# Two-part tokens evicted straight from PSUM: one change to a two-layer transformer kernel

## The chip, the cores and the metric

The kernel runs on one core of a Trainium2 chip. The metric is device time in microseconds (us) of one execution, as the median of several. TensorE (PE) multiplies and transposes and writes PSUM; ScalarE (ACT) and VectorE (DVE) read PSUM and SBUF; GpSimd (POOL) works on SBUF alone; SyncE (SP) issues most transfers.

## The reference

256 tokens of 1024 values pass through two layers, all in float32. The part that the change touches lies between the mixers and the experts. Each layer has a mixer (a block attention in the first layer, a compressed, selected and windowed attention, `nsa`, in the second), a feed-forward layer, a gated embedding term, and then a hybrid attention and a mixture of experts. Each of these begins with a norm:

```python
def _rms(x, g):
    xf = x.astype(F32)
    y = xf * lax.rsqrt(jnp.mean(xf * xf, axis=-1, keepdims=True) + RMS_EPS)
    return (y * g.astype(F32)).astype(x.dtype)
```

The feed-forward layer is down(silu(gate(y)) * up(y)) with 2816 hidden values. The embedding term adds sigmoid(y @ w_gate) * (p @ w_proj), where p holds 256 values per token.

## The kernel before, in words

The tokens are two tiles of 128 rows in `h` (tile t, 1024 columns). Products need the tokens the other way round, so each norm ends in a turn: `Norm.norm` writes the normed rows `xn`, and `Norm.turn(t)` lets TensorE transpose the eight 128-column chunks into two PSUM banks of four chunks each and evicts them with the gain.

A float32 product is made of three products of a shorter type: every operand is held in two parts, a high part and a low part (value minus high part). `mm3` (lines 329 to 331) multiplies high by high, high by low and low by high. For tokens these are the tiles XH and XL, written by `turn`. For weights, `Split` makes the parts: ScalarE casts a piece of 1024 columns into `whi` (line 193), and `Split.lows` subtracts it on an engine `second` into `wlo` (line 201). `Split.get(job)` hands out a piece; with `ahead` it first casts as many further pieces as there are free places (`pump`), and then it issues every low part that is pending. `second` is VectorE, but GpSimd within `ple` and for four pieces in layer 1's hybrid attention.

In `turn` before, ScalarE evicts bank 0 and VectorE bank 1, each in four instructions with the gain, back into `xn` as float32 (lines 378 and 382). ScalarE then casts chunks 0 and 1, 2 and 3, and 4 to 7 into XH (line 373), and VectorE subtracts the same three pieces into XL (line 386). Eight norms run through it, two tiles each, sixteen turns in all; the norms of the expert layers have no low part and keep their form.

The order of work is the order in which the program issues it: nothing reorders instructions of an engine, and each engine works through its own in order. The places of the sixteen turns:

- the start of the kernel (the first mixer's input, not normed: `raw`);
- `last_steps` of each mixer: the rest of the output product, then `ple_product` twice (the embedding's projection, twelve matmuls each, copied to `pv` by ScalarE at line 868), then both turns, and then the feed-forward layer with ten weight pieces cast and subtracted ahead;
- the end of `ffn` (tile 0) and the start of `ple` (tile 1);
- the end of `ple` (tile 0) and the start of what follows it (tile 1): the second mixer, or layer 0's hybrid attention;
- layer 1's hybrid attention (both).

`ple` is the gate block: for each tile eight pieces of product, at two of them a sigmoid on ScalarE (line 943), a multiplication with `pv` and an addition to `h` on VectorE (lines 946 and 390), the sums of squares on ScalarE (line 342) and at the end the norm.

In the second mixer's attention, `proj_steps` works a projection in four steps between units of attention; three of them fetch with `ahead`. In the hybrid attention, `halves` squares each half of the output on ScalarE and adds the second square to the first on GpSimd (line 1350).

Of the kernel before, what the change touches and what calls it, by code (L numbers as in the profile page):

```python
# [10 lines left out]
F32 = mybir.dt.float32  # L11
# [3 lines left out]
AF = mybir.ActivationFunctionType  # L15
ALU = mybir.AluOpType
# [3 lines left out]
D = 1024  # L20
# [133 lines left out]
class Split:  # L154


    def __init__(self, nc, ring, size):
        self.nc, self.ring, self.size = nc, ring, size
        self.jobs, self.at, self.made, self.free, self.low, self.pools = [], {}, {}, [], [], []
        self.second = nc.vector  # L160
        self.spare = 1

    def add(self, job, key, view, last):

# [8 lines left out]
    def make(self, spare=0):  # L173

        n = len(self.made)
        name, key, view, last = self.jobs[n]
        for pool, bufs, until, live in self.pools:
            while live and self.free[live[0]]:
                live.pop(0)
            if len(live) < bufs - spare and (until is None or n < self.at[until]):  # L180
                break
        else:
            return False
        live.append(n)
        src = view(self.ring.get(key))
        hi = pool.tile([128, self.size], F32R, name="whi", tag="whi", bufs=bufs)
        lo = pool.tile([128, self.size], F32R, name="wlo", tag="wlo", bufs=bufs)
        shape = [int(v) for v in src.shape[1:]]
        vh, vl = hi[:, :int(np.prod(shape))], lo[:, :int(np.prod(shape))]
        if len(shape) == 2:  # L190
            vh = vh.rearrange("p (a b) -> p a b", a=shape[0])
            vl = vl.rearrange("p (a b) -> p a b", a=shape[0])
        self.nc.scalar.copy(vh, src)  # L193
        self.made[name] = (vh, vl)
        self.low.append((self.second, vl, src, vh, key if last else None))
        return True

    def lows(self):

        for eng, vl, src, vh, key in self.low:  # L200
            eng.tensor_sub(vl, src, vh)  # L201
            if key:
                self.ring.done(key)
        self.low = []

    def pump(self, most=99):

# [3 lines left out]
    def get(self, job, ahead=True):  # L211
        while job not in self.made:
            assert self.make(), job
        if ahead:
            self.pump()
        self.lows()
        return self.made[job]

    def done(self, job):
# [41 lines left out]
def tile_kernel(ctx: ExitStack, tc: tile.TileContext, x, out, cat, sat, stop=None):  # L261
    nc = tc.nc
# [70 lines left out]
    class Norm:  # L333
# [26 lines left out]

        def turn(self, t, raw=False):
            src = h[:, t] if raw else self.xn[t]
            xn = tmp.tile([128, D], F32, name="xn", tag="xn") if raw else self.xn[t]
            pts = [wps(), wps()]
            for k in range(8):
                nc.tensor.transpose(pts[k // 4][:, 128 * (k % 4):128 * (k % 4) + 128], src[:, 128 * k:128 * k + 128], ident)

            to = [self.to[:, t, k] if self.low is None else xn[:, 128 * k:128 * k + 128] for k in range(8)]
            f_ = [slice(128 * c, 128 * c + 128) for c in range(4)]

            def parts(a, b):
                v = xn[:, 128 * a:128 * b].rearrange("p (c n) -> p c n", n=128)
                nc.scalar.copy(self.to[:, t, a:b], v)  # L373
                return self.low[:, t, a:b], v, self.to[:, t, a:b]

            lows = []
            for c in range(4):
                nc.scalar.activation(to[c], pts[0][:, f_[c]], AF.Copy, scale=self.gain[:, c:c + 1])
                if c % 2 and self.low is not None:
                    lows.append(parts(c - 1, c + 1))  # L380
            for c in range(4):
                nc.vector.tensor_scalar(to[4 + c], pts[1][:, f_[c]], self.gain[:, 4 + c:5 + c], None, ALU.mult)
            if self.low is not None:
                lows.append(parts(4, 8))
            for o, v, hi in lows:
                nc.vector.tensor_sub(o, v, hi)  # L386

    def add_half(t, b, v, nxt):
        hs = h[:, t, 512 * b:512 * b + 512]
# [93 lines left out]
    with ExitStack() as c1:  # L483
# [80 lines left out]
            plan_moe(l)  # L564


        def proj(name, b, nq, pair=None, skew=None, mid=None, bank=acc, ahead=True):


            o = [bank(), bank()]  # L570
            xh, xl = pair or (XH, XL)

            def piece(q, t):
                vh, vl = split.get((name, b, q), ahead)
                for c in range(2):
                    k = 2 * q + c
                    mm3(o[t], xh[:, t, k], xl[:, t, k], vh[:, c, :], vl[:, c, :], k == 0, k == 2 * nq - 1)

            if skew:
                for t in range(2):  # L580
                    for q in range(nq):
                        if q == nq - 1 and t == 0:
                            skew()
                        piece(q, t)
                        if q == nq - 1 and t and mid:
                            mid()
                        if t:
                            split.done((name, b, q))
                        if q % 2:
                            side.tick()  # L590
                    yield t, o[t]
                return
            for q in range(nq):
                for t in range(2):
                    piece(q, t)
                split.done((name, b, q))
                side.tick()
            yield 0, o[0]
            yield 1, o[1]

        def proj_steps(key, end):
# [259 lines left out]
                nc.vector.tensor_sub(pp[1][:, t], v, pp[0][:, t])  # L861
                yield 0

        def ple_product(i, b, pp, pv):

            for t, o in proj(f"pp{i}", b, 1, pp, bank=wps, ahead=False):
                pv[b, t] = keep.tile([128, 512], F32, name="pv", tag="pv", bufs=4)
                nc.scalar.copy(pv[b, t], o)

        def last_steps(i, outp, nxt, pp, pv):  # L870
            fns = [lambda: outp.finish(nxt, T1[10 + 6 * i]), lambda: ple_product(i, 0, pp, pv), lambda: ple_product(i, 1, pp, pv),
                   lambda: nxt.turn(0), lambda: nxt.turn(1)]
            for k in sorted(range(len(fns)), key=lambda k: T1[11 + 6 * i + k]):
                fns[k]()

        def ffn(i, nm, nxt):
            down = [[acc(), acc()] for _ in range(2)]
# [43 lines left out]
        def ple(i, nm, pv, nxt):  # L921

            seq = [(b, q) for b in range(2) for q in range(4)]
            split.second = nc.gpsimd
            for t in range(2):
                for n, (b, q) in enumerate(seq):
                    if t == 0 and n == T1[0]:
                        nm.turn(1)
                    if t and n == T1[1]:
                        nxt.turn(0)  # L930
                    if q == 0:
                        o = acc()
                    vh, vl = split.get((f"pg{i}", b, q), t == 0 or n < 6)
                    if n == T1[2]:
                        nxt.half(t, 0)
                    for c in range(2):
                        k = 2 * q + c
                        mm3(o, XH[:, t, k], XL[:, t, k], vh[:, c, :], vl[:, c, :], k == 0, k == 7)
                    if t:
                        split.done((f"pg{i}", b, q))  # L940
                    if q == 3:
                        sg = ptile([128, 512], F32, "sgp")
                        nc.scalar.activation(sg, o, AF.Sigmoid)
                        if b:
                            nc.scalar.preload_act_table_set(EXP)
                        nc.vector.tensor_mul(sg, sg, pv[b, t])
                        add_half(t, b, sg, b and nxt)
                nxt.norm(t)
            split.second = nc.vector

        rows_d = dram.tile([24, 383], F32, name="rows_d")
        cbias = keep.tile([128, 2, 16, 16], F32, name="cbias")
# [146 lines left out]
        def nsa(nm, nxt):  # L1099
# [140 lines left out]
            fill = proj_steps(("nsa", 1), lambda o: side.later(T1[6], lambda: side.spawn(second(o))))  # L1240
            side.later(T1[7], lambda: side.spawn(blocks(0)))
            att.hold()
            next(fill)
            for _ in att.start():
                next(fill)
                side.tick()
            att.run(AT1)
            side.drain()
            outp.chunk(6, (1,))
            last_steps(1, outp, nxt, pp, pv)  # L1250
# [18 lines left out]
    with ExitStack() as c2:  # L1269
# [41 lines left out]
        def mixer(l, qkv, sq, yh, yl):  # L1311
# [31 lines left out]
            def halves(br, c, y, gain, n):  # L1343

                if c == 0:
                    nc.scalar.activation(sq[:, br], y, AF.Square)
                else:
                    s_ = ptile([128, S], F32, "sqc", bufs=1)
                    nc.scalar.activation(s_, y, AF.Square)
                    nc.gpsimd.tensor_add(sq[:, br], sq[:, br], s_)  # L1350
                g = gain[:, c:c + 1]
                nc.scalar.activation(yh[:, br, c], y, AF.Copy, scale=g)
                yield n
                nc.vector.scalar_tensor_tensor(yl[:, br, c], y, g, yh[:, br, c], ALU.mult, ALU.subtract)
# [602 lines left out]
```

## Time and profile before

| | |
|---|---|
| median of 3 runs | 1916.67 us (1911.02 to 1917.64) |
| profiled execution | 1910.32 us, of it span 1908.5 us |
| mean granted TensorE clock | 0.974 of full speed |
| busy share of the span: PE, DVE, ACT, POOL | 93%, 42%, 35%, 4% |
| experts of the two layers | about 860 to 1315 and 1400 to 1908 us of the span |

In a row of a timeline stand the start and the duration in us, engine, line, operation, the tiles out<-in, their shape (partitions by elements) and the number of instructions joined in the row; in brackets is the idle time of the engine before it and what ended that. A row that joins several instructions gives the time from the first one's start to the last one's end. A row of a group gives the number of instructions, their busy time in us, the mean of one in ns, and the idle time ahead of them. A row of windows gives the stretch and its length, then for each engine (PE, its weight loads, DVE, ACT, POOL) busy us and instructions, then the granted clock, the busy share of the DMA queues and GB/s.

### The profile page before, as it was taken

How to read it: one execution, taken by the hardware profiler on the slowest of the kernel's cores; microseconds unless marked ns; L12 is line 12 of the kernel's file. 1: busy time of each engine (PE TensorE's matmuls, PEld its weight loads, DVE VectorE, ACT ScalarE, POOL GpSimd, SP SyncE). 2: the span in 40 equal slices, each digit the busy share in tenths (PEclk: the TensorE clock that was granted, in tenths of full speed). 3: DMA queues.
4: the chain of work that ended last, by engine and by line, in shares of the span. 5: the costliest groups of instructions: out<-in, count | busy, mean ns of one | idle time of the engine just before them, and what ended most of it. 6: DMA issues, size and time to landing. Idle time of an engine off the chain costs nothing. (4 is left out here: it accounts for less than half of the span.)

```text
span 1908.5 us, 25241 instructions
## 1 busy us (share of the span) xinstructions
PE 1777.5 (93%) x9983; PEld 1169.5 (61%) x9983; DVE 811.0 (42%) x1772; ACT 674.4 (35%) x1371; POOL 69.1 (4%) x92
## 2 busy tenths in 40 slices
PE   8998999898999999999999978997999999978996
PEld 6778999786689997874444443443874444433442
DVE  6667455767775556872111111113773111111112
ACT  6656445646574446651111110113552111110111
POOL 0000000300000003000000000001010000000000
PEclk9999999999999999999999989998998999998998
DMA  8437555442255554749999999999649999999996
GB/s 299 154 125 244 203 188 193 131 160 66 95 177 199 199 191 134 267 164 396 421 421 421 420 421 378 422 420 385 223 155 374 420 421 421 420 420 377 421 421 279
DMA packets 152908, 555.76 MB, mean 291 GB/s; under 512 B 9872, under 2 KB 69712, under 8 KB 103632
## 3 DMA queue, kind: packets, MB, share of 16 engines
q1 hardware_dynamic: 150672, 546.45, 73.9%
q0 software_dynamic: 2112, 7.63, 1.2%
q8 instruction: 81, 1.33, 0.3%
q14 instruction: 43, 0.35, 0.1%
HBM read 552.96 MB, written 1.09 MB: 290 GB/s over the span
## 5 line engine op out<-in xcount | busy, mean ns | idle before, releaser
L1745 PE MATMUL wps<-wring,h 128*64 128x512 f32 x1936 | 454.0, 596 | 10.6 <-DMA wring<-in_w_expert_up_dram 7.9
L1745 PEld LDWEIGHTS wps<-wring,h 128*64 128x64 f32 x1936 | 150.0, 138 | 287.3 <-issue 258.6
L201 DVE TENSOR_TENSOR wlo<-wring,whi 128x1024 fp32r<-128x1024 f32 (+1 forms) x273 | 288.3, 1094 | 73.6 <-ACT whi L193 73.3
L193 ACT CAST whi<-wring 128x1024 fp32r<-128x1024 f32 (+1 forms) x283 | 254.8, 945 | 23.0 <-PE acc L331 12.0
L329 PE MATMUL wps<-xh,whi 128*128 128x256 f32 x832 | 236.5, 284 | 4.7 <-ACT xh L373 4.7
L330 PE MATMUL wps<-xl,whi 128*128 128x256 f32 x832 | 234.8, 282 | 1.3 <-DVE xl L386 1.3
L331 PE MATMUL wps<-xh,wlo 128*128 128x256 f32 x832 | 234.5, 282 | 0.0
L1780 PE MATMUL wps<-wring,aT 128*64 128x512 f32 x984 | 227.4, 597 | 0.0
L1758 DVE SCALAR_TENSOR_TENSOR a<-wps,gs,a 128x256 f32<-128x256 f32 x64 | 28.0, 479 | 369.8 <-PE wps L1745 369.8
L329 PEld LDWEIGHTS wps<-xh,whi 128*128 128x128 f32 x832 | 157.5, 189 | 10.5 <-ACT xh L373 5.2
L1789 DVE SCALAR_TENSOR_TENSOR yl<-wps,gs,yh 128x512 fp32r<-128x512 f32 x64 | 47.9, 750 | 267.8 <-ACT yh L1788 263.9
L331 PEld LDWEIGHTS wps<-xh,wlo 128*128 128x128 f32 x832 | 160.3, 193 | 0.0
L330 PEld LDWEIGHTS wps<-xl,whi 128*128 128x128 f32 x832 | 157.5, 189 | 3.2 <-DVE xl L386 1.8
L329 PE MATMUL acc<-whi,xh 128*128 128x512 f32 (+1 forms) x360 | 146.6, 407 | 3.3 <-ACT whi L193 3.3
L1780 PEld LDWEIGHTS wps<-wring,aT 128*64 128x64 f32 x984 | 70.8, 137 | 128.4 <-issue 123.0
L331 PE MATMUL acc<-whi,xl 128*128 128x512 f32 (+1 forms) x360 | 141.3, 392 | 8.5 <-DVE xl L386 8.5
L330 PE MATMUL acc<-wlo,xh 128*128 128x512 f32 (+1 forms) x360 | 141.4, 393 | 2.3 <-DVE wlo L201 2.3
L1788 ACT ACTIVATE yh<-wps,gs 128x512 fp32r<-128x512 f32 x64 | 43.8, 687 | 262.9 <-PE wps L1780 212.2
L1769 ACT COPY aT<-wps 128x256 f32<-128x256 f32 x32 | 11.9, 372 | 239.7 <-PE wps L1768 239.7
L1755 ACT ACTIVATE a<-wps,gs 128x512 f32<-128x512 f32 x32 | 22.0, 688 | 179.9 <-PE wps L1745 179.9
L331 PEld LDWEIGHTS acc<-whi,xl 128*128 128x128 f32 x360 | 69.8, 194 | 24.9 <-DVE xl L386 10.2
L329 PEld LDWEIGHTS acc<-whi,xh 128*128 128x128 f32 x360 | 70.1, 195 | 18.1 <-ACT whi L193 4.6
(374 smaller groups left out, 2424.5 us busy)
## 6 DMA issues: line engine op xcount, KB each, us to landing
wring<-in_w_expert_down_dram SPq DMA_DIRECT2D x123, 1024.0 KB, 19.8
wring<-in_w_expert_up_dram SPq DMA_DIRECT2D x122, 1024.0 KB, 19.8
wring<-in_w_expert_gate_dram SPq DMA_DIRECT2D x120, 1024.0 KB, 19.8
wring<-in_w_ffn_gate_dram SPq DMA_DIRECT2D x22, 1024.0 KB, 9.1
wring<-in_w_ffn_up_dram SPq DMA_DIRECT2D x22, 1024.0 KB, 5.4
wring<-in_w_ffn_down_dram SPq DMA_DIRECT2D x22, 1024.0 KB, 7.4
wring<-in_w_in_dram SPq DMA_DIRECT2D x18, 1024.0 KB, 8.6
wring<-in_w_in_ab_dram SPq DMA_DIRECT2D x10, 1024.0 KB, 8.7
```

The costliest lines, as they stand in the source:

```text
L193: self.nc.scalar.copy(vh, src)
L201: eng.tensor_sub(vl, src, vh)
L329: nc.tensor.matmul(o, lh, rh, start=start, stop=False)
L330: nc.tensor.matmul(o, lh, rl, start=False, stop=False)
L331: nc.tensor.matmul(o, ll, rh, start=False, stop=stop)
L1745: nc.tensor.matmul(o[i][64 * ab:64 * ab + 64, :], xg[:, k, at:at + 64], ws[ab][:, c, :], start=k == 0, stop=k == 7)
L1755: nc.scalar.activation(a, o[0], AF.Silu, scale=r)
L1758: nc.vector.scalar_tensor_tensor(a[:, s_], o[1][:, s_], r, a[:, s_], ALU.mult, ALU.mult)
L1769: (nc.vector.tensor_copy if hf else nc.scalar.copy)(aT[:, 2 * hf:2 * hf + 2], pt[:, 256 * hf:256 * hf + 256].rearrange("p (j n) -> p j n", ...
L1780: nc.tensor.matmul(y[d2][64 * ab:64 * ab + 64, :], aT[:, 2 * hf + j, 64 * ab:64 * ab + 64], ws[ab][:, j, 512 * d2:512 * d2 + 512], start=h ...
L1788: nc.scalar.activation(ys[0][:, s_], y[d2], AF.Copy, scale=g)
L1789: nc.vector.scalar_tensor_tensor(ys[1][:, s_], y[d2], g, ys[0][:, s_], ALU.mult, ALU.subtract)
```

## The change

`turn` no longer goes through `xn`. For every chunk ScalarE evicts bank to XH with the gain, rounded to the high part, and VectorE takes the same chunk of the bank once more, multiplies it by the gain, subtracts the high part and writes XL:

```diff
-            for c in range(4):
-                nc.scalar.activation(to[c], pts[0][:, f_[c]], AF.Copy, scale=self.gain[:, c:c + 1])
-                if c % 2 and self.low is not None:
-                    lows.append(parts(c - 1, c + 1))
...
+            for c in range(8):
+                v = pts[c // 4][:, 128 * (c % 4):128 * (c % 4) + 128]
+                g, to = self.gain[:, c:c + 1], self.to[:, t, c]
+                if self.low is not None:
+                    nc.scalar.activation(to, v, AF.Copy, scale=g)
+                    nc.vector.scalar_tensor_tensor(self.low[:, t, c], v, g, to, ALU.mult, ALU.subtract)
+                elif c < 4:
+                    nc.scalar.activation(to, v, AF.Copy, scale=g)
+                else:
+                    nc.vector.tensor_scalar(to, v, g, None, ALU.mult)
```

In `last_steps` the order of the products stays, and turn 0 is issued between the two tiles' matmuls of the last one (`proj` gets a parameter `between` for that):

```diff
-            fns = [lambda: outp.finish(nxt, T1[10 + 6 * i]), lambda: ple_product(i, 0, pp, pv), lambda: ple_product(i, 1, pp, pv),
-                   lambda: nxt.turn(0), lambda: nxt.turn(1)]
-            for k in sorted(range(len(fns)), key=lambda k: T1[11 + 6 * i + k]):
-                fns[k]()
+            outp.finish(nxt, T1[10 + 6 * i])
+            ple_product(i, 1 - i, pp, pv)
+            ple_product(i, i, pp, pv, lambda: nxt.turn(0))
+            nxt.turn(1)
```

```diff
             for q in range(nq):
                 for t in range(2):
                     piece(q, t)
+                    if between and t == 0:
+                        yield 0, o[0]
+                        between()
```

The low parts of the gate blocks' pieces go to VectorE, and so do the hybrid attention's added squares:

```diff
         def ple(i, nm, pv, nxt):
-            split.second = nc.gpsimd
...
-            split.second = nc.vector
```

```diff
                     nc.scalar.activation(s_, y, AF.Square)
-                    nc.gpsimd.tensor_add(sq[:, br], sq[:, br], s_)
+                    nc.vector.tensor_add(sq[:, br], sq[:, br], s_)
```

In the second mixer's attention `split.late` is set from before the first step of the projection until the attention has run. A fetch with it issues the low parts that were pending before it looked ahead, and leaves those of the pieces that it has just cast to the next fetch. `make` also issues pending low parts first where the piece's weights are not in the ring yet:

```diff
     def get(self, job, ahead=True):
         while job not in self.made:
             assert self.make(), job
+        n = len(self.low) if self.late else None
         if ahead:
             self.pump()
-        self.lows()
+        self.lows(n)
```

## Rows read from the trace of the kernel before

**Rows 1.** Windows of the span: busy us by engine, granted clock, DMA share, GB/s

```profile
525.00:545.00 20.00, 17.11 (x88) 15.03 (x87) 16.32 (x33) 17.16 (x38) 0.38 (x2) 0.83 0.10 30
```

**Rows 2.** Groups by shape over the span: xcount, busy us, mean ns, idle before

```profile
L378 ACT ACTIVATE xn<-wps,sm 128x128 f32<-128x128 f32 x48 | 15.0, 363 | 10.7 <-PE wps L366 10.7
L382 DVE TENSOR_SCALAR xn<-wps,sm 128x128 f32<-128x128 f32 x48 | 13.5, 343 | 11.7 <-PE wps L366 11.5
L1354 DVE SCALAR_TENSOR_TENSOR yl<-wps,sm,yh 128x256 fp32r<-128x256 f32 x8 | 3.8, 478 | 0.0
L201 POOL TENSOR_TENSOR wlo<-wring,whi 128x1024 fp32r<-128x1024 f32 x10 | 26.4, 2661 | 10.9 <-DVE xn L352 8.2 <-ACT whi L193 2.6
L1350 POOL TENSOR_TENSOR sq<-sq,sqc 128x256 f32<-128x256 f32 x12 | 10.3, 857 | 114.8 <-ACT sqc L1349 114.8
```

**Rows 3.** Timeline of ACT and DVE, of ACT and PE: engines sharing a bank

```profile
380.76 1.07 ACT L1067 COPY c2k<-wps 64x512 f32<-64x512 f32 x2 [1.70 <-PE wps L1065]
381.37 0.69 DVE L1069 COPY c2k<-wps 64x508 f32<-64x508 f32 x1 [1.06 <-ACT c2k L1067]
...
907.50 0.37 ACT L1769 COPY aT<-wps 128x256 f32<-128x256 f32 x1 [7.46 <-PE wps L1768]
907.92 0.50 PE L1768 MATMUL wps<-idg,a 128*128 128x128 f32 x2 [0.46 <-ACT aT L1769]
```

**Rows 4.** Timeline of PE, ACT and DVE in the first last steps

```profile
139.56 0.40 PE L329 MATMUL wps<-whi,ph 128*128 128x512 f32 x1
140.95 1.91 PE L366 MATMUL wps<-idg,xn 128*128 128x128 f32 x16
141.15 0.59 ACT L868 COPY pv<-wps 128x512 f32<-128x512 f32 x1 [0.81 <-PE wps L331]
144.09 0.62 ACT L378 ACTIVATE xn<-wps,sm 128x128 f32<-128x128 f32 x2
146.54 9.63 ACT L193 CAST whi<-wring 128x1024 fp32r<-128x1024 f32 x10
145.20 0.38 PE L329 MATMUL wps<-xh,whi 128*128 128x256 f32 x1 [2.34 <-ACT xh L373]
147.62 11.44 DVE L201 TENSOR_TENSOR wlo<-wring,whi 128x1024 fp32r<-128x1024 f32 x10 [0.26 <-ACT whi L193]
159.88 0.50 PE L329 MATMUL acc<-whi,ah 128*128 128x512 f32 x1 [2.50 <-ACT ah L905]
```

**Rows 5.** Timeline of DVE, the same place of the second mixer

```profile
539.40 11.45 DVE L201 TENSOR_TENSOR wlo<-wring,whi 128x1024 fp32r<-128x1024 f32 x10 [0.25 <-ACT whi L193]
```

**Rows 6.** Timeline of PE, first matmul of the kernel

```profile
9.50 0.80 PE L329 MATMUL acc<-whi,xh 128*128 128x512 f32 x1 [2.81 <-ACT whi L193]
```

**Rows 7.** Timeline of PE, POOL, DVE and PE: the first gate block

```profile
335.24 0.50 PE L331 MATMUL acc<-whi,xl 128*128 128x512 f32 x1 [0.78 <-DVE xl L386]
351.48 10.65 POOL L201 TENSOR_TENSOR wlo<-wring,whi 128x1024 fp32r<-128x1024 f32 x4 [4.18 <-DVE xn L352]
357.14 2.78 DVE L390 TENSOR_TENSOR h<-h,sgp 128x512 f32<-128x512 f32 x1
360.88 4.67 DVE L386 TENSOR_TENSOR xl<-xn,xh 128x256 fp32r<-128x256 f32 x3
362.46 0.50 PE L331 MATMUL acc<-whi,xl 128*128 128x512 f32 x1 [3.20 <-DVE xl L386]
369.40 1.11 PE L366 MATMUL wps<-idg,xn 128*128 128x128 f32 x8 [1.40 <-DVE xn L352]
```

**Rows 8.** Timeline of PE, second gate block, then the start of layer 1's hybrid

```profile
754.96 0.50 PE L331 MATMUL acc<-whi,xl 128*128 128x512 f32 x1 [3.86 <-DVE xl L386]
1330.09 0.49 PE L329 MATMUL acc<-whi,xh 128*128 128x512 f32 x1 [0.52 <-ACT whi L193]
```

**Rows 9.** Timeline of DVE and PE in the second mixer's attention

```profile
444.18 1.23 DVE L201 TENSOR_TENSOR wlo<-wring,whi 128x1024 fp32r<-128x1024 f32 x1 [2.10 <-ACT whi L193]
447.27 2.20 PE L674 MATMUL wps<-kwT,qT 64*128 64x256 f32 x8 [3.31 <-DVE m L690]
```

More of the change, by code (lines that the diff above doesn't have):

```diff
@@ L161, in __init__ @@
         self.spare = 1
+        self.late = False
     def add(self, job, key, view, last):
@@ L176, in make @@
         name, key, view, last = self.jobs[n]
+        if key not in self.ring.tiles:
+            self.lows()
         for pool, bufs, until, live in self.pools:
@@ L196, in make, with lows @@
         return True
-    def lows(self):
-        for eng, vl, src, vh, key in self.low:
+    def lows(self, n=None):
+        now, self.low = self.low[:n], [] if n is None else self.low[n:]
+        for eng, vl, src, vh, key in now:
             eng.tensor_sub(vl, src, vh)
@@ L203, in lows @@
                 self.ring.done(key)
-        self.low = []
     def pump(self, most=99):
@@ L362, in turn @@
             src = h[:, t] if raw else self.xn[t]
-            xn = tmp.tile([128, D], F32, name="xn", tag="xn") if raw else self.xn[t]
             pts = [wps(), wps()]
@@ L366, in turn @@
                 nc.tensor.transpose(pts[k // 4][:, 128 * (k % 4):128 * (k % 4) + 128], src[:, 128 * k:128 * k + 128], ident)
[L368 to L376, printed above, removed]
-            for c in range(4):
-                nc.scalar.activation(to[c], pts[0][:, f_[c]], AF.Copy, scale=self.gain[:, c:c + 1])
-                if c % 2 and self.low is not None:
-                    lows.append(parts(c - 1, c + 1))
[L381 to L386, printed above, removed]
+            for c in range(8):
[8 more added lines that the diff above has]
+                    nc.vector.tensor_scalar(to, v, g, None, ALU.mult)
     def add_half(t, b, v, nxt):
@@ L564, in tile_kernel, with proj @@
             plan_moe(l)
-        def proj(name, b, nq, pair=None, skew=None, mid=None, bank=acc, ahead=True):
+        def proj(name, b, nq, pair=None, skew=None, mid=None, bank=acc, ahead=True, between=None):
             o = [bank(), bank()]
@@ L595, in proj @@
                     piece(q, t)
+                    if between and t == 0:
+                        yield 0, o[0]
+                        between()
                 split.done((name, b, q))
                 side.tick()
-            yield 0, o[0]
+            if not between:
+                yield 0, o[0]
             yield 1, o[1]
@@ L862, in ple_inputs, with ple_product @@
                 yield 0
-        def ple_product(i, b, pp, pv):
-            for t, o in proj(f"pp{i}", b, 1, pp, bank=wps, ahead=False):
+        def ple_product(i, b, pp, pv, between=None):
+            for t, o in proj(f"pp{i}", b, 1, pp, bank=wps, ahead=False, between=between):
                 pv[b, t] = keep.tile([128, 512], F32, name="pv", tag="pv", bufs=4)
@@ L1242, in nsa @@
             att.hold()
+            split.late = True
             next(fill)
@@ L1247, in nsa @@
             att.run(AT1)
+            split.late = False
             side.drain()
```

## The prediction

> **What bounds the kernel now.** I read four views, in this order. The windows say that TensorE is busy nine tenths of the span up to the experts and that the transfers are not the limit where the change works; in the stretch of the second last steps they use 0.10 of the queues and the granted clock falls to 0.83, which lies between TensorE's two levels, so part of it ran at 1.2 GHz [rows 1]. So a microsecond that TensorE loses or gains before the experts should reach the end. The list of who TensorE waits for then names the norm's parts: the xh casts, the xl subtractions and the normed rows ahead of them. The timeline around these waits gives the order: transposes, ScalarE and VectorE on one bank each, the casts and lows, the first matmul [rows 4, 6 to 8]. Last, the groups by shape give prices [rows 2].
>
> **The turn, the part that decides.** Before, one `turn` had ScalarE read bank 0 in four instructions and VectorE bank 1 in four, side by side; ScalarE came to its next work 2.45 us after its first eviction (144.09 for the second turn, the weight casts from 146.54) [rows 4]. After, each of the eight 128-column chunks is read by ScalarE (high part) and then by VectorE (low part, which needs the high part), so both engines read both banks. The data alone would let ScalarE go on to chunk 1 while VectorE reads chunk 0. The question is whether a shared bank lets them. Two places of the trace have engines sharing one. VectorE's copy L1069 waits 1.06 us and starts at 381.37, 0.61 after the first of ScalarE's two copies L1067, though the two read different partition halves and neither needs the other's result (that both write one tile could be the reason as well). TensorE's two transposes at 907.92 wait 0.46 us for ScalarE's read of the other half of their bank and start 0.05 us after it has ended [rows 3]. I take it that the two engines take turns on a bank.
>
> The Trainium skill ("PSUM — Partial Sum Buffer", section "PSUM bank collisions raise a hardware error") speaks against this change: two engines on one bank and one quarter of the partitions at one time are an error, two reads included, and the compiler's scheduler orders them. The trace agrees as far as those two waits go; it has no pair of ScalarE and VectorE reads on all 128 partitions. By this rule the sum is the one below, without it that of the first rival.
>
> Then a chunk costs ScalarE's 363 ns, VectorE's 343 (the 128-column tensor_scalar; the new operation takes 478 out of PSUM at twice the columns, 135 more, which I read as the same price at 128) and two handovers of 0.04 (between 0.03 and 0.05): 0.79 us [rows 2, 3]. Four chunks of a bank are done by VectorE 3.1 us after the turn's start; at the change of bank ScalarE runs ahead once, so chunk 4 is done at 3.37, chunk 7 at 5.73. ScalarE ends at 5.35 and its next instruction can start at about 5.25, not 2.45: **2.8 us later per turn**; VectorE is held for some 2.5 longer. Bounds of that per turn: minus 0.4 (no taking turns: eight evictions at ScalarE's own pitch, 0.26 from two in 0.62 [rows 4], 2.1 us) and plus 3.5 (handovers of 0.1).
>
> What this does place by place, of the sixteen turns:
> - Start of the kernel: the first matmul at 9.50 waits for a weight cast [rows 6] that stands behind the turn on ScalarE: **plus 2.8**. The second turn there lies beside the products of the first tile: 0, at most half a microsecond.
> - First last steps: turn 0 moves ahead of the last six matmuls, so its transposes start at 139.56, not 140.95 [rows 4]; the evictions can start some 0.7 later (in the rows they follow the copy of 141.15, 0.59 long, behind transposes of 140.95), at 140.3, with VectorE coming from the normed rows shortly after. ScalarE is through at about 145.6. The copy of the last product (0.5) stands behind these evictions on ScalarE, turn 1's second bank waits for that copy, and turn 1 starts at 146.05. The ten weight casts follow at 151.3, before at 146.54: plus 4.8. VectorE's ten lows (147.62 plus 11.44) are fed by these casts, and the first down product at 159.88 waits behind the lows [rows 4]. So **plus 4.8**. TensorE is fed its first gate at 0.79 a chunk, which ends before that.
> - Second last steps: the same, less 0.4: there the lows end at 550.85, the activation behind them some 0.8 later, and TensorE comes to its first down product only about 0.3 after that [rows 5] (the 0.8 is 159.88 less the end of the lows there [rows 4]): **plus 4.4**.
> - First gate block: here the change removes something. Four of the ten lows on GpSimd took 10.65 us [rows 7] at 2661 ns each [rows 2], and beside them VectorE's three subtractions took 4.67 us; the product at 362.46 waits 3.20 for them. On VectorE a low costs 1.14 (ten in 11.44), so four cost 4.6, about what GpSimd's disturbance cost it. The first matmul of the block (0.78 of waiting at 335.24 [rows 7]) gets its chunk sooner. But three turns lie on one chain from the end of the feed-forward layer: turn, add to h, norm, turn 1, sigmoid, add, norm, turn 0, sigmoid, add, norm, and the transposes at 369.40, which already wait 1.40 for that chain [rows 7]. Three turns would add 8.2; VectorE gains back the subtractions, which go, and most of the 2.78 that one 512-column add took beside GpSimd at 357.14, some 5 in sum, and pays the four lows in gaps where it waited for ScalarE. I come to the normed rows for 369.40 about 3.0 late: **plus 3.0**, bounds minus 4 (only the waits go) and plus 5.
> - Second gate block: the same chain, but the transposes at its end do not wait, so the 3.86 of the wait at 754.96 [rows 8] is some cushion: the same step comes 1.2 late there, the chain behind it **plus 2.6**, bounds minus 4.5 and plus 5.
> - Layer 1's hybrid: the chunks keep up with TensorE at its slow pace, but the adds and the norm that lead to the weight casts, for which 1330.09 waits [rows 8], come later by ScalarE's casts and GpSimd's low behind the turn: **plus 1.8**, bounds minus 1 and plus 3.
>
> **The other edits.** Low parts held back in attention: VectorE's low at 444.18 waits 2.10 for its cast with the scores queued behind it, and TensorE's wait of 3.31 at 447.27 follows from them [rows 9]. Held back to the next fetch, the cast is done when the low's turn comes: **minus 2.0**, bounds minus 2.5 and 0. Five tiles are split ahead, so the low is not late. Squares on VectorE: twelve adds of 857 ns leave GpSimd [rows 2]; on VectorE one costs some 0.4 (478 for a heavier operation of that size), and GpSimd no longer slows it as at 360.88: **minus 0.3**, bounds plus and minus 1.5. The guard in `make` and the written-out order of the last steps issue nothing new: 0.
>
> **Sum.** 2.8 + 4.8 + 4.4 + 3.0 + 2.6 + 1.8 - 2.0 - 0.3 = plus 17.1. The profiled execution took 1910.32 (span 1908.5 and 1.8 around it), which gives 1927.4; it is the fastest of the four times shown, 0.33% under the median of 1916.67, from which the same step gives 1933.8. I forecast 1931.
>
> **The rivals.**
> - Both engines read a bank together (not slower, but faster). Then the waits go: 3.2 + 0.8 and about 1 of slow matmuls at the first gate block, 3.9 + 1.5 at the second, 1.5 and 1.8 at the last steps, 1 in layer 1, 2 in attention, 0.7 elsewhere: minus 17, 1897 to 1900. It decides at one point: does ScalarE's second chunk start while VectorE reads the first? For it: no data runs that way. Against it: rows 3.
> - Taking turns, but hidden at the gate blocks: the chain there has room (table loads, casts, the block's own products), so both blocks gain their waits (minus 3.2 and minus 3.9) and only the start, the last steps and layer 1 pay: 13.8 - 7.1 - 2.3 = plus 4.4, 1915 to 1921, no measurable change.
> - Taking turns, and the clock falls. At 0.79 a chunk TensorE works half the time, and waits of 2 to 5 us stand ahead of it; in [rows 1] that is where the clock was 0.83. After 362.46 nine matmuls ran at half pace, 1.8 us lost. Four or five such places more: plus 25, 1935 to 1942.
>
> **How the numbers follow.** Forecast 0.58, clock 0.22, hidden at the gates 0.12, both engines at once 0.08. Within half a per cent (9.6 us, about what a measurement of this kernel can tell from no change) lies most of the third and little of the others: same 0.12, faster 0.07, slower 0.81. The range leaves out the fast rival and the edges: 1916 to 1944.
>
> **What would show it.** In the changed turn VectorE's eight low parts should stand 0.79 us apart, each ScalarE eviction but the fifth waiting for VectorE; the casts of the first last steps should start about 5 us later against the transposes; GpSimd should have no low in the gate blocks and the waits behind them should have turned into waits for normed rows. ScalarE's evictions at 0.27 apart would make the forecast wrong, and so would the transposes of 369.40 coming earlier than before.

## The result and the profile after

The changed kernel takes 1932.12 us (median of 4 runs, 1931.31 to 1934.68), the kernel before 1913.85 in the same comparison: a ratio of 1.0102, 95% interval 1.0085 to 1.0119, some 18 us or 1.0% slower. The profiled execution has a span of 1929.6 us, 21.1 more than before; the mean granted clock is 0.973 against 0.974, so averaged over the span the clock hardly differs.

The turn first. These are ScalarE, and then VectorE, in the second turn of the first last steps of the changed kernel (`turn` now evicts on lines 374 and 375; lines behind it stand 3 earlier):

```profile
149.09 0.38 ACT L374 ACTIVATE xh<-wps,sm 128x128 fp32r<-128x128 f32 x1
149.89 0.37 ACT L374 ACTIVATE xh<-wps,sm 128x128 fp32r<-128x128 f32 x1 [0.42 <-DVE xl L375]
150.68 0.37 ACT L374 ACTIVATE xh<-wps,sm 128x128 fp32r<-128x128 f32 x1 [0.42 <-DVE xl L375]
151.46 0.63 ACT L374 ACTIVATE xh<-wps,sm 128x128 fp32r<-128x128 f32 x2 [0.42 <-DVE xl L375]
...
154.35 9.57 ACT L196 CAST whi<-wring 128x1024 fp32r<-128x1024 f32 x10
...
149.50 0.35 DVE L375 SCALAR_TENSOR_TENSOR xl<-wps,sm,xh 128x128 fp32r<-128x128 f32 x1 [0.40 <-ACT xh L374]
150.29 0.35 DVE L375 SCALAR_TENSOR_TENSOR xl<-wps,sm,xh 128x128 fp32r<-128x128 f32 x1 [0.43 <-ACT xh L374]
151.08 0.35 DVE L375 SCALAR_TENSOR_TENSOR xl<-wps,sm,xh 128x128 fp32r<-128x128 f32 x1 [0.44 <-ACT xh L374]
151.87 0.61 DVE L375 SCALAR_TENSOR_TENSOR xl<-wps,sm,xh 128x128 fp32r<-128x128 f32 x2 [0.44 <-ACT xh L374]
```

Each engine's idle time of 0.40 to 0.44 ends with the other's instruction: ScalarE's second chunk waits for VectorE's read of the first, though it needs nothing of it. Chunks are 0.79 us apart; the one pair that is not (x2 in 0.63) is the change of bank. The wait stands in the program: in the trace 96 of the 128 evictions of the sixteen turns, six in each turn, carry a wait on the semaphore (a counter that one engine raises and another waits for) that VectorE's low parts raise. So what is measured here is the price of that order; whether the chip by itself would make the two engines take turns, no run here shows. The weight casts start 5.26 us after the turn's first eviction, where it was 2.45 [rows 4]. The groups by shape of the whole span show twelve of the sixteen turns (the gain of the other four lies in another tile):

```profile
L374 ACT ACTIVATE xh<-wps,sm 128x128 fp32r<-128x128 f32 x96 | 34.0, 367 | 43.8 <-DVE xl L375 35.6 <-PE wps L369 8.2
L375 DVE SCALAR_TENSOR_TENSOR xl<-wps,sm,xh 128x128 fp32r<-128x128 f32 x96 | 32.5, 349 | 39.7 <-ACT xh L374 39.6
```

ScalarE spends 34.0 us in these evictions and 35.6 us waiting for VectorE's reads between them. The single prices are 367 and 349 ns, where 363 and 343 were assumed from [rows 2].

TensorE's places in the changed kernel that answer to [rows 4, 6, 7], and the last transposes of the second gate block, in order of time:

```profile
12.18 0.79 PE L333 MATMUL acc<-whi,xh 128*128 128x512 f32 x1 [5.51 <-ACT whi L196]
149.52 0.38 PE L333 MATMUL wps<-xh,whi 128*128 128x256 f32 x1 [2.32 <-ACT xh L374]
167.68 0.54 PE L333 MATMUL acc<-whi,ah 128*128 128x512 f32 x1 [2.76 <-ACT ah L902]
370.74 0.49 PE L335 MATMUL acc<-whi,xl 128*128 128x512 f32 x1 [0.86 <-DVE xl L375]
381.32 1.97 PE L369 MATMUL wps<-idg,xn 128*128 128x128 f32 x8 [6.26 <-DVE xn L356]
785.13 1.40 PE L369 MATMUL wps<-idg,xn 128*128 128x128 f32 x8 [2.50 <-DVE xn L356]
```

The kernel's first matmul comes 2.7 us later, the first down product (159.88 before) 7.8 later. At the first gate block the wait of 3.20 has become 0.86, as meant, but the transposes behind it wait 6.26 for normed rows, where they waited 1.40, and the same transposes of the second gate block wait 2.50, where they did not wait in the kernel before:

```profile
763.16 1.04 PE L366 MATMUL wps<-idg,xn 128*128 128x128 f32 x8
```

Windows of the changed kernel show what comes next: ahead of and behind the matmul of 167.68, and then behind the wait of 6.26:

```profile
164.00:168.00 4.00, 1.24 (x10) 1.02 (x9) 3.53 (x5) 2.38 (x4) 0.00 (x0) 1.00 1.04 333
168.00:172.00 4.00, 4.00 (x12) 3.09 (x11) 2.16 (x3) 1.91 (x3) 0.00 (x0) 0.57 1.04 386
381.00:384.00 3.00, 2.68 (x11) 2.49 (x12) 1.41 (x4) 0.74 (x2) 0.00 (x0) 0.50 0.54 187
```

Behind these two waits TensorE's next matmuls run at half clock for some 4 us. The clock fell once more, at the end of the first last steps' second turn, where the kernel before had it in full. The changed kernel, then the kernel before:

```profile
150.00:154.00 4.00, 4.00 (x17) 3.44 (x18) 1.96 (x6) 1.99 (x6) 0.00 (x0) 0.62 0.00 0
```

```profile
147.00:151.00 4.00, 4.00 (x38) 4.00 (x37) 3.74 (x4) 4.00 (x5) 0.00 (x0) 1.00 0.00 0
```

The delay against the kernel before, taken from the same matmuls in both traces, grows like this:

| stretch | grows by | forecast |
|---|---|---|
| start, to 60 us | +3.1 | +2.8 |
| first last steps, to the first down product | +4.7 | +4.8 |
| behind it | +1.4 | none |
| end of the feed-forward layer, first gate block, to its last transposes | +2.7 | +3.0 |
| behind them | +2.2 | none |
| second mixer's attention | -0.8 | -2.0 |
| second last steps, to the first down product | +4.4 | +4.4 |
| behind it | +1.5 | none |
| second gate block, to its last transposes | +2.7 | +2.6 |
| behind them | +1.6 | none |
| layer 0's hybrid attention | -1.0 | -0.15 |
| layer 1's start, to the matmul of 1330.09 | +1.7 | +1.8 |
| behind it, with the hybrid attention | -3.1 | -0.15 |
| both layers' experts | 0.0 | none |
| sum | +21.1 | +17.1 |

### The profile page after: what moved, and what is told of

The parts are those of the page before. It is cut to its first block, busy times and chain, and to the rows that moved or that the text cites. A ratio compares the mean times of both kernels' runs of the same rounds, so it can differ in the third digit from the quotient of the medians.

```text
span 1929.6 us, 25258 instructions
## 1 busy us (share of the span) xinstructions
PE 1786.3 (93%) x9983; PEld 1171.0 (61%) x9983; DVE 812.9 (42%) x1810; ACT 677.8 (35%) x1387; POOL 32.3 (2%) x70
## 5 line engine op out<-in xcount | busy, mean ns | idle before, releaser
L205 DVE TENSOR_TENSOR wlo<-wring,whi 128x1024 fp32r<-128x1024 f32 (+1 forms) x283 | 299.5, 1097 | 65.4 <-ACT whi L196 65.0
```

## The experiments

**The bank or something else.** The first two keep every instruction of the change and alter only the order within a turn.

```diff
+            def parts(c, low):
...
+            if self.low is not None:
+                for b in range(2):
+                    for low in range(2):
+                        for c in range(4 * b, 4 * b + 4):
+                            parts(c, low)
+                return
             for c in range(8):
```

With low 0, `parts` issues ScalarE's eviction of chunk c, with low 1 VectorE's low part of it.

> The changed kernel with one thing else in the turn: ScalarE evicts the four chunks of a bank one after the other, then VectorE takes its four low parts of that bank while ScalarE does the other bank. Same instructions, same data. Theory (the engines take turns on a bank): ScalarE is through after 2.1 to 2.3 us instead of 5.3, VectorE after 3.4 instead of 5.7; the start, the last steps and the gate blocks all gain, about 14 us under the kernel before, 1896 to 1904. Rival (the loss comes from the other edits, lows on VectorE or the moved turn): it stays at 1925 or more.

Measured: 1892.41 against 1911.91 for the kernel before, ratio 0.990 (0.988 to 0.992); faster than forecast, and some 40 us under the changed kernel. A second set of runs gave 1891.20, ratio 0.9898 (0.9882 to 0.9915).

> The turn by bank once more, on the same chip as the kernel with the fill, for the comparison: 1890 to 1895, some 1.0% under the kernel before.

ScalarE and then VectorE in the first last steps of this kernel, both turns:

```profile
141.74 2.18 ACT L376 ACTIVATE xh<-wps,sm 128x128 fp32r<-128x128 f32 x8
143.75 0.65 ACT L879 COPY pv<-wps 128x512 f32<-128x512 f32 x1
144.22 2.26 ACT L376 ACTIVATE xh<-wps,sm 128x128 fp32r<-128x128 f32 x8
146.23 9.85 ACT L196 CAST whi<-wring 128x1024 fp32r<-128x1024 f32 x10
...
142.92 2.16 DVE L374 SCALAR_TENSOR_TENSOR xl<-wps,sm,xh 128x128 fp32r<-128x128 f32 x8 [0.63 <-ACT xh L376]
145.47 2.16 DVE L374 SCALAR_TENSOR_TENSOR xl<-wps,sm,xh 128x128 fp32r<-128x128 f32 x8 [0.39 <-ACT xh L376]
147.55 11.44 DVE L205 TENSOR_TENSOR wlo<-wring,whi 128x1024 fp32r<-128x1024 f32 x10
```

Eight evictions in 2.18 to 2.26 us and eight low parts in 2.16, with no instruction waiting inside a turn (in this trace one of the 128 evictions carries a wait on VectorE's semaphore); VectorE's first low part comes 1.2 us after ScalarE's first eviction, when ScalarE has left the bank.

```diff
-            for c in range(8):
+            for c in ((0, 4, 1, 5, 2, 6, 3, 7) if self.low is not None else range(8)):
```

> The changed kernel with the chunks in the order 0 4 1 5 2 6 3 7, ScalarE and VectorE issued in turn as in the changed kernel, so that neighbouring chunks lie in different banks. Theory (bank): ScalarE's evictions come 0.40 us apart, a turn takes 3.5 us, about 1903 to 1911. Rival (what costs is the handover from ScalarE to VectorE chunk by chunk, whatever the bank): evictions stay 0.79 apart on average and the time stays at 1930 to 1934.

Measured: 1902.71, ratio 0.995 (0.9934 to 0.9967). Here the engines are issued in turn just as in the changed kernel, and each low part still needs its high part; only neighbouring chunks lie in different banks. The same two turns:

```profile
142.59 3.11 ACT L374 ACTIVATE xh<-wps,sm 128x128 fp32r<-128x128 f32 x8
146.07 3.16 ACT L374 ACTIVATE xh<-wps,sm 128x128 fp32r<-128x128 f32 x8
146.49 3.13 DVE L375 SCALAR_TENSOR_TENSOR xl<-wps,sm,xh 128x128 fp32r<-128x128 f32 x8 [0.39 <-ACT xh L374]
```

A chunk every 0.40 us instead of 0.79. So neither the handover nor the order of issue costs the 0.79: it is the order that the program's waits keep between two engines on one bank. Each bank of a turn is also one tile of the program; which of the two the waits go by, no run here separates.

**The turn or the other edits.** One kernel has all of the change but the turn, the other nothing of the change but the turn.

```diff
         def turn(self, t, raw=False):
...
-                    nc.vector.scalar_tensor_tensor(self.low[:, t, c], v, g, to, ALU.mult, ALU.subtract)
...
+            for o, v, hi in lows:
+                nc.vector.tensor_sub(o, v, hi)
```

> The changed kernel with the turn of the kernel before; all other edits stay. Theory: the other edits are gains by themselves, the gate blocks lose their waits of 3.2 and 3.9, the last steps about 0.9 each: 1899 to 1908. Rival (the other edits cost the time): 1920 or more.

Measured: 1898.22, ratio 0.9931 (0.9905 to 0.9957). The other edits gain 13 to 14 us by themselves.

```diff
         def turn(self, t, raw=False):
...
-            for o, v, hi in lows:
-                nc.vector.tensor_sub(o, v, hi)
...
+                    nc.vector.scalar_tensor_tensor(self.low[:, t, c], v, g, to, ALU.mult, ALU.subtract)
...
```

> The kernel before with the changed turn alone. Theory: all of the loss and more, because the last steps now have two long turns in a row (6 each) and the gate blocks keep GpSimd's lows: 1936 to 1946. Rival (the other edits cost the time): 1910 to 1918.

Measured: 1942.49, ratio 1.0164 (1.0147 to 1.0181): the turn alone costs 31 us, and the other edits take back about 10 of them in the changed kernel. By the same matmuls as in the table, its gate blocks lose 8.0 and 6.8 where the changed kernel loses 4.9 and 4.3, so GpSimd's low parts were worth removing there too; the second mixer's attention loses 1.9 where the changed kernel gains 0.8.

**The other edits, one by one, on the turn by bank.** Each of these kernels takes back one edit from the kernel of the first experiment.

```diff
...
-            ple_product(i, i, pp, pv, lambda: nxt.turn(0))
-            nxt.turn(1)
+            fns = [lambda: outp.finish(nxt, T1[10 + 6 * i]), lambda: ple_product(i, 0, pp, pv), lambda: ple_product(i, 1, pp, pv),
+                   lambda: nxt.turn(0), lambda: nxt.turn(1)]
...
```

> The turn by bank with the last steps as before (both products, then both turns). Theory: the moved turn is worth about 1.4 us per mixer, the six matmuls that cover its start, and 0.5 of the copy: 2.5 to 4 us slower than the turn by bank, about 1895.5. Rival (TensorE waits there for the weights' low parts, which come when they come): no difference.

Measured: 1892.86, the same. The time is the rival's, its reason is not: in both mixers the first gate product and the first down product come 0.9 us later without the moved turn. But behind the first down product this kernel keeps the full clock, and gains 1.6 and 1.5 us on the turn by bank, which does not (below). So the moved turn gains 0.9 a mixer, and in these two executions the clock takes it back.

```diff
             seq = [(b, q) for b in range(2) for q in range(4)]
+            split.second = nc.gpsimd
...
                 nxt.norm(t)
+            split.second = nc.vector
```

> The turn by bank with the gate blocks' ten low parts back on GpSimd. Theory (GpSimd's work slows VectorE's beside it, and the turn's low parts wait for that): the waits of 3.2 and 3.9 come back in part, 5 to 8 us slower than the turn by bank, 1897 to 1901. Rival (the new turn has taken the subtractions of SBUF data away and reads PSUM, so GpSimd no longer matters): 0 to 2.

Measured: 1898.36, 6 slower, as expected; in the profiled execution, the slowest of the four, the first gate block loses 5.1 us and the second 1.3, and another 2.9 are lost ahead of both, in stretches that the edit does not touch.

```diff
             att.hold()
-            split.late = True
```

> The turn by bank without the held-back low parts in attention. In the changed kernel 2.1 us were gained at the score matmul of 447 and most of it lost again by 470. Theory (later units are bound by another chain): 0.5 to 1 us slower. Rival (the prediction's term): 2 us slower.

Measured: 1893.76, 1.4 slower in the medians, within what these runs scatter (1889.82 to 1895.25). In the traces the score matmul comes 2.1 us later, at the end of the attention 2.3 are left, and behind the next last steps 0.9. So the forecast's 2.0 is right for the attention itself. What is lost again is the clock's in this pair of executions: TensorE waits as long for the second layer's first down product here (2.47 us) as in the turn by bank (2.48), but behind it this kernel keeps the full clock, where the turn by bank runs at half. Behind that wait, first here and then in the turn by bank:

```profile
547.00:551.00 4.00, 3.58 (x19) 3.00 (x20) 2.76 (x3) 2.65 (x4) 0.00 (x0) 1.00 1.05 389
```

```profile
545.00:549.00 4.00, 4.00 (x11) 3.06 (x12) 2.48 (x3) 2.19 (x3) 0.00 (x0) 0.57 1.05 387
```

```diff
-                    nc.vector.tensor_add(sq[:, br], sq[:, br], s_)
+                    nc.gpsimd.tensor_add(sq[:, br], sq[:, br], s_)
```

> The turn by bank with the twelve added squares back on GpSimd. Theory (GpSimd's 0.86 slows VectorE's work beside it, and TensorE waits for VectorE in the hybrid attention): 1.0 to 2.5 us slower, as the changed kernel won 1.0 in layer 0's. Rival (the prediction's small term): 0.3 slower.

Measured: 1899.86, 7.5 slower: more than either expected. The trace puts only 1.9 of it in the two hybrid attentions (1.06 and 0.85), where VectorE's scaling takes longer beside GpSimd's add and TensorE waits for it. VectorE without and with that add beside it:

```profile
795.26 1.23 DVE L1398 TENSOR_TENSOR X<-X,l 128x1024 f32<-128x1024 f32 x1
```

```profile
797.86 1.69 DVE L1398 TENSOR_TENSOR X<-X,l 128x1024 f32<-128x1024 f32 x1
797.74 0.74 POOL L1361 TENSOR_TENSOR sq<-sq,sqc 128x256 f32<-128x256 f32 x1 [4.91 <-ACT sqc L1360]
```

The other 7 of the two profiled executions stand in stretches where both programs are the same and TensorE's granted clock was lower in one of them (0.88, 0.93 and 0.85 against 1.00, 1.00 and 0.95 in the windows 366 to 380, 470 to 516 and 1310 to 1345). This is no chance of one execution: all four of this kernel's are slower than all of the turn by bank, at a mean clock of 0.973 to 0.976 against 0.977 to 0.981. What sends the clock there, and whether the edit has to do with it, is open; so only the 1.9 is taken as the shown price of the edit.

**What is lost behind the first down product.** In the changed kernel TensorE waits 2.76 us there, and the next eight matmuls of 512 columns run 0.43 apart instead of 0.23; the windows above have the granted clock at 0.57. The turn by bank shows the same in both layers, the kernel before in neither: there TensorE waits 2.50 us in the first layer and not at all in the second. In the next kernel TensorE has work in the wait.

```diff
+                if j == 1:
+                    fill = wps()
+                    for k in range(24):
+                        nc.tensor.transpose(fill[:, 128 * (k % 4):128 * (k % 4) + 128], ident, ident)
                 if 0 < j <= n - LATE:
                     emit_down(j - 1, (0, 1))
```

> The turn by bank, and 24 transposes of the identity into an unused bank (2.8 us of TensorE) ahead of the first down product of each feed-forward layer, where TensorE waits 2.8 us; nothing reads them. Theory (the 1.4 to 1.5 us lost behind that wait in each layer is the clock, which falls after the wait): the clock stays up, the down product comes at most 0.3 later, 2 to 3 us faster than the turn by bank. Rival (the first down products are slow for another reason, their operands): no faster, up to 0.6 slower.

Measured: 1892.77 against 1891.20, no difference. In the trace the theory holds where it speaks: the slow matmuls are gone in both layers, and 1.3 and 1.4 us against the kernel without the fill with them; the first down product comes no later. Second layer, the fill, the first three matmuls and a window behind it; then the same place without it:

```profile
541.57 2.78 PE L922 MATMUL wps<-idg 128*128 128x128 f32 x24
544.21 0.50 PE L333 MATMUL acc<-whi,ah 128*128 128x512 f32 x1
544.54 0.40 PE L334 MATMUL acc<-wlo,ah 128*128 128x512 f32 x1
544.77 0.40 PE L335 MATMUL acc<-whi,al 128*128 128x512 f32 x1
...
544.00:548.00 4.00, 4.00 (x24) 3.33 (x23) 1.80 (x3) 2.33 (x4) 0.00 (x0) 1.00 1.05 377
```

```profile
542.80 0.50 PE L333 MATMUL acc<-whi,ah 128*128 128x512 f32 x1 [2.76 <-ACT ah L916]
543.13 0.45 PE L334 MATMUL acc<-wlo,ah 128*128 128x512 f32 x1
543.38 0.63 PE L335 MATMUL acc<-whi,al 128*128 128x512 f32 x1
543.81 0.63 PE L333 MATMUL acc<-whi,ah 128*128 128x512 f32 x1
...
543.00:547.00 4.00, 4.00 (x11) 3.06 (x11) 2.83 (x4) 2.02 (x3) 0.00 (x0) 0.57 1.05 389
```

But this execution lost 0.7 us at the start, 1.3 in the first mixer and 1.6 in the first gate block, where nothing had been changed, so the gain does not show in the whole. So in this place it is the clock; a gain of the whole kernel is not shown.

## Why the prediction was right

The time (1931 forecast, 1932.12 measured) and its main step hold: the engines take turns on a bank, at 0.79 us a chunk and 2.8 us a turn. What [rows 3] had suggested, the second experiment shows, which excludes the handover and the order of issue as the cause. What makes the engines wait the trace shows too: a semaphore, in the program's order. Of the two waits of [rows 3] the first, between copies that read different halves of the partitions and write one tile, could not tell a bank from a tile. The start, both last steps and both gate blocks came to within 0.3 us of their terms, since there the delay of ScalarE's and VectorE's chain runs straight to a matmul that waits for it.

What was off, and cancelled in part, so that a time within 1 us of the forecast is partly luck:

- The clock, which I had kept out of the sum as a rival of its own, belonged into it. It did fall in the turns at 0.79 a chunk, as I had argued, but cost next to nothing there: in the first last steps TensorE ran its first gate products at 0.62 instead of 1.00, and then still waited 0.76 us for a low part and 2.76 at the first down product. It cost time behind the waits that the turns made: at the two first down products and the two gate blocks' last transposes, 1.4 + 2.2 + 1.5 + 1.6 = 6.7 us. The rival's price (1.8 a place, four or five places) was right, its place was not. That this is the clock, the windows and the lengths of the matmuls show; that work in the wait prevents it, the fill shows for the first down products alone.
- The gate blocks' chains came as forecast (2.7 and 2.7), including the low parts that VectorE now issues ahead of the third turn. (Three turns of 2.8 are 8.4, not 8.2; with that the term would be some 0.2 larger.)
- Layer 1's start had its 1.7, at a wait of 2.57 us for a weight cast just ahead of the matmul that stood at 1330.09 before. But it was given back and more: the matmuls behind 1330.09 had run at half clock before and ran at full clock here. Which of the two a stretch gets I had no way to forecast.
- In attention the 2.0 came (2.4 us were gained by 474), and then 1.6 went again, to the clock once more: the changed kernel ran at 0.66 from 474 to 479 us, the kernel before at 1.00 in the same matmuls (462 to 467). The squares gave about 1 us a layer, not 0.3 together: what they had cost was VectorE's slower work beside GpSimd (1.69 us against 1.23), and not the add.
- By the profiled executions the loss is 21.1 and not the 18.3 of the medians, because the one profiled before was among its quickest. So 1931 lies close to the median with a sum 4 us too small: the clock's 6.7 and 1.2 of the attention are missing, and the two hybrid attentions were 0.9 and 3 too dear.

The rival of both engines reading one bank at once did not come true in any run. Its sum was about right, though, for the order that lets them read two banks at once: minus 17 forecast, minus 20 measured by bank. Its largest terms came nearly as named: the gate blocks gained 5.6 and 6.7 us (5.0 and 5.4 forecast), the last steps up to the first down product 1.6 and 1.9 (1.5 and 1.8).

## What to carry to other kernels

Where two engines must read the same PSUM data, count a bank as one resource: give the second engine the bank when the first is through with all of it, not chunk by chunk. The instructions were right here and their order alone was worth 40 us, so look for idle times of some 0.4 us that end with the other engine's read, and ask whether the program's own waits made them. A kernel with one bad edit can hide good ones: test edits apart before the whole is thrown away.

## What the runs showed of the hardware

- A chain ScalarE, VectorE on one bank hands over in 0.03 to 0.05 us each way, by semaphore; 0.79 per 128 columns is nearly all execution (367 and 349 ns). Alone and back to back on a bank, eight evictions take 2.18 us and eight low parts 2.16, 0.26 apart.
- The clock fell to half behind waits of 2.46 to 2.77 us for the first down product in the changed kernel and the turn by bank, but not behind one of 2.50 in the kernel before and one of 2.77 in the turn by bank with the old last steps. Without the held-back low parts one execution has both: half clock behind a wait of 2.48 in the first layer, full clock behind one of 2.47 in the second. So the length of the wait alone does not decide it.
- A stretch whose program is the same in two kernels differed by up to 2.8 us through the clock alone (470 to 516 us with the squares on GpSimd, 0.93 against 1.00 in the turn by bank), which sets what one profile can tell of a small edit.
- VectorE's product of 128x1024 values took 1.23 us alone and 1.69 beside a GpSimd add of 0.74.
